# Heads transposed in pairs in a sparse-attention decoder layer, with copies to the other partitions by GpSimd

## The chip, the cores and the metric

One core of a Trainium2 chip runs the kernel. The metric is the device time of one execution in microseconds (us); three executions were timed, and one more was profiled. TensorE is named PE in the profile (PEld its weight loads), VectorE DVE, ScalarE ACT, GpSimd POOL and SyncE SP.

## The reference

One layer on 2048 prompt tokens (16 blocks of 128) and 64 sample tokens, all in float32. Cut to what matters here:

```
z = rmsnorm(x) @ w_in                    # 1024 -> 3656 columns, split into:
q, k, v (8, 4, 4 heads x 64), qi (8 index heads x 64), ki (64), wi (8), ga, u, vm, gm
score[t, l] = sum_h wi[t, h] * relu(qi[t, h] . ki[l])      # causal
idx = top_k(score, 256)                                    # per query
o = softmax(q . k[idx] / 8) @ v[idx];   attn = o * silu(ga)
gm = gelu(u) * (W_s @ layernorm(gelu(vm)) + b) * silu(gm)  # in chunks of 128
r = x + concat(attn, gm) @ w_out
y = r + sigmoid(rmsnorm(r) @ w_ple_gate) * (p @ w_ple_proj)
```

The sample tokens have their keys and values in paged caches. k, v, ki and the sample's normalised vm rows are outputs too.

## The kernel before

float32 products are made of two fp32r parts: `split` has ScalarE copy the value from PSUM into a high part (L124) and VectorE write the rest into a low part (L125). Keys are stacked on the partitions: for 64 dimensions, partitions 0 to 63 hold the high part and 64 to 127 the low part (`ki` for the index, `Kst` for attention). A query head must then lie on both halves. The kernel gets this by doubling before the transpose: each head of 64 columns is loaded twice side by side (`load_qi` for the index, L659; `load_q` for attention, L999), or copied twice by ScalarE (`twice`, L1015, for keys), so that one transpose per head of 128x128 puts it on both halves (L673 for index heads, L1036 for queries, L1021 for keys). Two PSUM tiles of four heads take the eight heads of a block.

The kernel has three phases.

Phase A does the input projection in three rounds of blocks ([0-4 and the sample], [5-10], [11-15]); a round goes through 14 column chunks of w_in and, in each chunk, through its blocks (`proj`, L312 to L322; two PSUM buffers "z"; `post` evacuates them on ScalarE and VectorE). In the first round raw weights are loaded into 5 buffers "raw" (L282), and split by GpSimd ("whi", L288) and VectorE ("wlo", L289); the parts are stored and reloaded in the later rounds. After each product `pump` gives out some steps of index work, within a credit in units of 128 keys: `idx` (queries' transposes, then per 1024 keys and head two matmuls into "dots", a relu on ScalarE L691 and an accumulation on VectorE L693 into "big", which GpSimd first sets to a small descending ramp from a constant `iota`, L679), and `topk`: seven evaluations of a threshold (ScalarE counts over the row, L829; VectorE corrects the threshold, L833 to L849), then VectorE passes over a row and a mask that goes to memory. At most two top-ks and one block of dots are open; the block behind is "primed": its loads are issued. The gMLP half of the output product follows (`gm_product`, L579 to L583, weights "whi" by L302), and in the middle of it (u == 9) the rest of the index work is given out, the pools of the projections are closed, and `prep_early` prepares queries and keys for phase B in between; its transposes use the same two PSUM buffers "tp" as `gm_split` (L567).

Phase B is the attention: blocks 0 to 15, four key heads g each; scores (L1103, L1104), mask and running minimum on VectorE (L1105), exponentials on ScalarE (L1112), transposes of the probabilities (L1138), their split (L124, L125), values (L1155). `prep_q` of the next block runs after g == 2, and the load of the one after that follows it. The sample's attention is interleaved.

Phase C is the output product and the gate. Its weights are loaded and split first (`raw_split`): of the gate's ten parts, GpSimd makes the high part of every third (L1423), and the low part of every third (L1424).

The order within a queue is not the order in which the program gives instructions out: a scheduler places each instruction on its engine's queue by a simulated time line when its operands and buffers are there, with the order of the program as priority. Each engine then works through its queue in that order.

## Time and profile before

| | |
|---|---|
| timed executions | 1889.49, 1889.77, 1900.7 us (median 1889.77) |
| profiled execution | 1893.5 us, of it the span of the core 1891.7 us |
| mean granted clock of TensorE | 0.988 of 2.4 GHz |
| busy: TensorE, VectorE, ScalarE, GpSimd | 1833.5, 1242.1, 1018.2, 623.5 us |
| moved by DMA | 261.53 MB, 83176 of 243806 packets under 512 B |
| phase A, B, C (begin, us) | 0, 1045, 1532 |

The profile is one execution on the chip. "Busy" of TensorE is modelled, since matmuls are pipelined: a duration of 273 ns does not mean that the next one starts 273 ns later. The chain is the work that ended last, followed back from the end. A wait is put down to the instruction that came last.

### The profile page before, as it was taken

What the parts mean: (1) busy time and instruction counts of PE and PEld (TensorE: products, weight loads), DVE (VectorE), ACT (ScalarE), POOL (GpSimd) and SP (SyncE); (2) the same over time, 40 slices, a digit from 0 to 9 for tenths busy, and PEclk for the clock granted to TensorE, in tenths of its full rate; (3) what the DMA queues carried; (4) which work ended last, traced back from release to release, by engine and by line L of the source; (5) the groups of instructions that cost most, each with busy time, mean ns of one, the idle gap of its engine ahead of it and who ended that gap; (6) DMA issues with size and microseconds to landing.
All of it is one profiled execution on the core that took longest, in us unless ns stands there. A gap on an engine that the chain in (4) does not pass through costs nothing.

```text
span 1891.7 us, 33962 instructions
## 1 busy us (share of the span) xinstructions
PE 1833.5 (97%) x11974; PEld 1601.0 (85%) x11974; DVE 1242.1 (66%) x3631; ACT 1018.2 (54%) x1909; POOL 623.5 (33%) x950
## 2 busy tenths in 40 slices
PE   7989998999999999999988899999999999999998
PEld 7989988999999999999877678778777777888887
DVE  5597665378878547788752789888999764233321
ACT  4244335256565636766654888868788653122121
POOL 5482562342012324013303442233221364222221
PEclk9989999999999999999999899999999999999999
DMA  8855756645344554554553442233220373223211
GB/s 253 247 163 179 223 189 203 215 131 161 119 162 146 194 174 145 163 170 134 176 188 128 134 112 76 64 108 94 61 78 12 100 258 122 74 95 104 94 37 45
DMA packets 243806, 261.53 MB, mean 138 GB/s; under 512 B 83176, under 2 KB 209840, under 8 KB 243248
## 3 DMA queue, kind: packets, MB, share of 16 engines
q1 hardware_dynamic: 237744, 240.45, 40.5%
q0 software_dynamic: 5888, 18.88, 3.4%
q8 instruction: 95, 1.56, 0.3%
q14 instruction: 79, 0.65, 0.1%
HBM read 171.90 MB, written 87.37 MB: 137 GB/s over the span
## 4 chain that ended last, share of the span: by engine, by line
PE 83%; DVE 5%; DMA 5%; POOL 2%; issue 2%; ACT 2%; SPq 0%; DVEq 0%; POOLq 0%; ACTq 0%
PE z L319 10%; PE z L320 10%; PE z L322 10%; PE b_o L1155 7%; PE b_tp L1138 6%; PE c_mm L1471 5%; PE c_mm L1470 5%; PE c_mm L1474 5%; PE b_s L1103 3%; PE dots L688 3%; PE dots L689 3%; PE b_s L1104 3%; PE z L579 1%; PE z L580 1%; PE z L583 1%
## 5 line engine op out<-in xcount | busy, mean ns | idle before, releaser
L319 PE MATMUL z<-whi,hhi 128*128 128x256 f32 (+1 forms) x1792 | 463.0, 292 | 10.5 <-ACT vt L414 5.0
L320 PE MATMUL z<-wlo,hhi 128*128 128x256 f32 (+1 forms) x1792 | 454.1, 287 | 0.2 <-DVE wlo L289 0.2
L319 PEld LDWEIGHTS z<-whi,hhi 128*128 128x128 f32 x1792 | 341.9, 191 | 21.2 <-issue 8.5
L320 PEld LDWEIGHTS z<-wlo,hhi 128*128 128x128 f32 x1792 | 341.8, 191 | 6.1 <-DVE wlo L289 1.5
L322 PE MATMUL z<-whi,hlo 128*128 128x256 f32 (+1 forms) x1792 | 262.6, 286 | 0.0
L322 PEld LDWEIGHTS z<-whi,hlo 128*128 128x128 f32 x1792 | 237.7, 190 | 2.0
L693 DVE SCALAR_TENSOR_TENSOR big<-dots,sgn,big 128x1024 f32<-128x1024 f32 (+7 forms) x176 | 179.2, 1018 | 52.3 <-ACT dots L691 50.6
L125 DVE TENSOR_TENSOR b_pt<-b_tp,b_pt 128x512 fp32r<-128x512 f32 (+1 forms) x288 | 183.4, 655 | 12.1 <-ACT b_pt L124 11.0
L691 ACT ACTIVATE dots<-dots 128x1024 f32<-128x1024 f32 (+7 forms) x176 | 140.3, 801 | 87.7 <-PE dots L689 82.9
L1155 PE MATMUL b_o<-b_pt,Vst 128*128 128x512 f32 x544 | 184.1, 424 | 1.2 <-DVE b_pt L125 0.8
L124 ACT ACTIVATE b_pt<-b_tp 128x512 fp32r<-128x512 f32 (+1 forms) x288 | 155.5, 578 | 48.2 <-PE b_tp L1138 45.4
L1138 PE MATMUL b_tp<-mats,b_sm 128*128 128x128 f32 x1088 | 172.0, 275 | 2.3 <-DVE b_pt L125 1.8
L1112 ACT ACTIVATE b_sm<-b_sm,b_st 128x128 f32<-128x128 f32 (+15 forms) x128 | 154.7, 1210 | 16.2 <-DVE b_st L1105 15.4
L829 ACT ACTIVATE bfw<-big,tk 128x384 bf16<-128x384 f32 (+14 forms) x105 | 136.4, 1300 | 45.7 <-DVE tk L849 27.9
L1138 PEld LDWEIGHTS b_tp<-mats,b_sm 128*128 128x128 f32 x1088 | 131.5, 141 | 34.1 <-ACT b_sm L1112 4.8
L1103 PE MATMUL b_s<-Kst,b_qh 128*128 128x512 f32 (+3 forms) x320 | 139.5, 439 | 4.1 <-DVE b_st L1105 2.2
L1105 DVE CUSTOM_DVE_ANT_0 b_sm<-b_s,b_mask,b_st 128x512 f32<-128x512 f32 (+3 forms) x192 | 123.9, 646 | 22.6 <-PE b_s L1104 17.8
L1104 PE MATMUL b_s<-Kst,b_ql 128*128 128x512 f32 (+3 forms) x320 | 117.6, 370 | 0.0
L688 PE MATMUL dots<-ki_stack,qih 128*128 128x512 f32 (+3 forms) x304 | 113.0, 373 | 3.1 <-DVE mk L833 3.1
L689 PE MATMUL dots<-ki_stack,qil 128*128 128x512 f32 (+3 forms) x304 | 110.2, 371 | 0.0
L1471 PE MATMUL c_mm<-c_l_w_ple_gate,c_mh 128*128 128x512 f32 x272 | 106.7, 392 | 3.2 <-DVE c_l_w_ple_gate L1424 2.1
L1470 PE MATMUL c_mm<-c_h_w_ple_gate,c_mh 128*128 128x512 f32 x272 | 109.0, 401 | 0.0
(351 smaller groups left out, 3747.0 us busy)
## 6 DMA issues: line engine op xcount, KB each, us to landing
whi<-s_wh SPq DMA_DIRECT2D x52, 512.0 KB
wlo<-s_wl SPq DMA_DIRECT2D x52, 512.0 KB
raw<-w_in SPq DMA_DIRECT2D x112, 128.0 KB
s_wh<-whi SPq DMA_DIRECT2D x13, 1024.0 KB
s_wl<-wlo SPq DMA_DIRECT2D x13, 1024.0 KB
b_qr<-s_q SPq DMA_DIRECT2D x32, 256.0 KB
s_r<-hlo SPq DMA_DIRECT2D x32, 256.0 KB
c_r<-s_r SPq DMA_DIRECT2D x16, 512.0 KB
```

The lines of the kernel that those rows point to most:

```text
L125: nc.vector.tensor_tensor(lo, src, hi.bitcast(F32), OP.subtract)
L319: nc.tensor.matmul(z, lhsT=hh[:, k], rhs=wh[:, k, :n], start=(k == 0), stop=False)
L320: nc.tensor.matmul(z, lhsT=hh[:, k], rhs=wl[:, k, :n], start=False, stop=False)
L322: nc.tensor.matmul(z, lhsT=hl[:, k], rhs=wh[:, k, :n], start=False, stop=(k == 7))
L688: nc.tensor.matmul(ps[:, s0:s0 + sn], lhsT=qh[h // 4][:, h % 4], rhs=rhs, start=True, stop=False)
L693: nc.vector.scalar_tensor_tensor(a, r, self.sgn[:, b, h:h + 1], a, op0=OP.mult, op1=OP.add)
L1103: nc.tensor.matmul(ps, lhsT=qh[:, h], rhs=rhs, start=True, stop=False)
L1104: nc.tensor.matmul(ps, lhsT=ql[:, h], rhs=rhs, start=False, stop=True)
L1138: nc.tensor.transpose(ps[:, k, r], sm2[r][:, (k0 + k) * 128:(k0 + k) * 128 + 128], ident)
L1155: nc.tensor.matmul(o.rearrange("p a b -> p (a b)"), lhsT=Vst[:, kb, g].rearrange("p a d -> p (a d)"), rhs=pt[:, k].rearrange("p a b -> p ( ...
L1470: nc.tensor.matmul(z, lhsT=hi[:, k], rhs=wts[k][0][:, ns], start=(k == 0), stop=False)
L1471: nc.tensor.matmul(z, lhsT=hi[:, k], rhs=wts[k][1][:, ns], start=False, stop=(b == SB and k == nk - 1))
```

## The change

1. Index queries (`idx`), attention queries (`prep_q`) and keys (`prep_kv`) are loaded once, and two heads of 64 are transposed together (one 128x128 transpose; head 2j on partitions 0 to 63, head 2j+1 on 64 to 127). `heads` splits each half where it lies, and then GpSimd copies it to the other half (four copies of 64 x 512). For query blocks 0 to 4 (`direct`) ScalarE and VectorE write the other half from PSUM as well. For keys, the high part is written on the head's own half and the low part on the other; `twice` is gone. Head h is now `[:, h % 2, h // 2]`.
2. The index queries of the primed block are transposed and split once the running block has done five steps, at no credit. `prep_q` runs after g == 0.
3. When only top-ks are left, their steps take no credit, so `pump` gives them all out at once.
4. The ramp is made for each block by GpSimd's iota and a scaling in place; the constant is gone. "raw" has 4 buffers, and the index key of a token is written once.
5. `prep_early` uses the PSUM buffers "dots". In phase C the gate's weights are split by ScalarE and VectorE alone.

```diff
-            rp = pool("a_raw", 5)
+            rp = pool("a_raw", 4)
...
+                    kin = wk.tile([128, 64], F32, name="kin", bufs=KIN)[:P]
+                    nc.scalar.activation(kin, z[:, 0:64], AF.Copy, scale=rs)
+                    self.rope(nc.vector, kin[:, None, :], rt, 1, wk, P)
...
+                        nc.tensor.transpose(ps[:64, 0], kin, ident)
+                        kst = self.ki[:, b]
+                        nc.scalar.activation(kst[0:64], ps[:64, 0], AF.Copy)
+                        nc.vector.tensor_tensor(kst[64:128], ps[:64, 0], kst[0:64].bitcast(F32), OP.subtract)
+
+                    if b != SB:
+                        later.append(ki_t)
...
+                    if primed and primed[0][0] not in ready and (not dots or steps[0] >= 5):
+                        ready.add(primed[0][0])
+                        if primed[0][0] != SB:
+                            next(primed[0][1])
...
-                            credit[0] -= v
+                            if dots or primed or blocks_due:
+                                credit[0] -= v
...
-                            early = self.prep_early(eb, lambda: self.tp.tile([128, 4, 128], F32, name="tp"))
+                            early = self.prep_early(eb, lambda: self.dp.tile([128, 1024], F32, name="dots")[:, :512]
+                                                    .rearrange("p (a b) -> p a b", a=4))
...
+    def order(self, acc, P):
+        nc = self.nc
+        nc.gpsimd.iota(acc[:P], pattern=[[1, acc.shape[1]]], base=0, channel_multiplier=0,
+                       allow_small_or_imprecise_dtypes=True)
+        nc.gpsimd.tensor_scalar(acc[:P], acc[:P], -UNIT, 1.0, op0=OP.mult, op1=OP.mult)
+
+    def heads(self, pool, names, ps, bufs, direct=False):
+        nc = self.nc
+        qh, ql = (pool.tile([128, 2, 4, 128], F32R, name=n, bufs=bufs) for n in names)
+        own = [slice(0, 64), slice(64, 128)]
+        for e in range(2):
+            nc.scalar.activation(qh[own[e], e], ps[own[e]], AF.Copy)
+            nc.vector.tensor_tensor(ql[own[e], e], ps[own[e]], qh[own[e], e].bitcast(F32), OP.subtract)
+            if direct:
+                nc.scalar.activation(qh[own[1 - e], e], ps[own[e]], AF.Copy)
+                nc.vector.tensor_tensor(ql[own[1 - e], e], ps[own[e]], qh[own[e], e].bitcast(F32), OP.subtract)
+        if direct:
+            return qh, ql
+        for t in (qh, ql):
+            for e in range(2):
+                nc.gpsimd.tensor_scalar(t[own[1 - e], e], t[own[e], e].bitcast(F32), 1.0, 1.0, op0=OP.mult, op1=OP.mult)
+        return qh, ql
+
...
     def idx(self, b):
         nc, wk, wk2 = self.nc, self.wk, self.wk2
         W = 128 * (b + 1)
-        qds = self.load_qi(b)
+        qd = wk2.tile([128, 4, 128], F32, name="qid", bufs=2)
+        nc.sync.dma_start(qd, self.s_qi[b].rearrange("p (h d) -> p h d", h=4))
         yield None
-        qh, ql = [], []
-        for j in range(2):
-            qd = qds[j].rearrange("p h a d -> p h (a d)")
-            ps = self.tp.tile([128, 4, 128], F32, name="tp")
-            for h in range(4):
-                nc.tensor.transpose(ps[:, h], qd[:, h], self.ident)
-            qh.append(wk2.tile([128, 4, 128], F32R, name="qih", bufs=3))
-            ql.append(wk2.tile([128, 4, 128], F32R, name="qil", bufs=3))
-            self.split(qh[j], ql[j], ps)
-            yield 2
+        ps = self.tp.tile([128, 4, 128], F32, name="tp")
+        for j in range(4):
+            nc.tensor.transpose(ps[:, j], qd[:, j], self.ident)
+        qh, ql = self.heads(wk2, ("qih", "qil"), ps, 2)
+        yield None
         acc = self.big.tile([128, SEQ], F32, name="big")[:, :W]
-        nc.gpsimd.tensor_scalar(acc, self.iota[:, :W], -UNIT, 1.0, op0=OP.mult, op1=OP.mult)
+        self.order(acc, 128)
...
-            q = io.tile([128, 8, 2, 64], F32, name="b_qr", bufs=1)
+            q = io.tile([128, 4, 128], F32, name="b_qr", bufs=1)
             ga = io.tile([128, 512], F32, name="b_ga")
-            for a in range(2):
-                nc.sync.dma_start(q[:, :, a], self.s_q[i].rearrange("t (h d) -> t h d", h=8))
+            nc.sync.dma_start(q, self.s_q[i].rearrange("t (h d) -> t h d", h=4))
...
-        kds = {}
-
-        def twice(i):
-            kds[i] = raw.tile([128, 4, 2, 64], F32, name="b_kd")
-            nc.scalar.copy(kds[i], kvs[i][0].rearrange("p (h d) -> p h d", h=4)[:, :, None, :].to_broadcast([128, 4, 2, 64]))
-
         def prep_kv(i, psum):
-            k, v = kds.pop(i), kvs.pop(i)[1]
+            k, v = kvs.pop(i)
             ps = psum()
-            for g in range(4):
-                nc.tensor.transpose(ps[:, g], k[:, g].rearrange("p a d -> p (a d)"), ident)
-            ks = Kst[i // 4][:, :, (i % 4) * 128:(i % 4) * 128 + 128]
-            nc.scalar.activation(ks, ps, AF.Copy)
-            V.tensor_tensor(ks[64:128], ps[64:128], ks[64:128].bitcast(F32), OP.subtract)
+            for j in range(2):
+                nc.tensor.transpose(ps[:, j], k[:, j * 128:j * 128 + 128], ident)
+            ks = Kst[i // 4].rearrange("p (j e) n -> p j e n", e=2)[:, :, :, (i % 4) * 128:(i % 4) * 128 + 128]
+            own = [slice(0, 64), slice(64, 128)]
+            for e in range(2):
+                nc.scalar.activation(ks[own[e], :, e], ps[own[e], 0:2], AF.Copy)
+                V.tensor_tensor(ks[own[1 - e], :, e], ps[own[e], 0:2], ks[own[e], :, e].bitcast(F32), OP.subtract)
...
+            ps = psum()
+            for j in range(4):
+                nc.tensor.transpose(ps[:, j], q[:, j], ident)
+            qh, ql = self.heads(qp, ("b_qh", "b_ql"), ps, 2, direct=i < 5)
...
-                if si < len(steps) and g == 2 and at + 1 < NB:
+                if si < len(steps) and g == 0 and at + 1 < NB:
...
-                    raw_split(*gates[q], nc.gpsimd if q % 3 == 2 else nc.scalar, nc.gpsimd if q % 3 == 1 else V)
+                    raw_split(*gates[q], nc.scalar, V)
```

## Rows read from the trace of the kernel before

**Rows 1.** The page: TensorE's busy time, and the chain that ended last by engine.

```profile
PE 1833.5 (97%) x11974; PEld 1601.0 (85%) x11974; DVE 1242.1 (66%) x3631; ACT 1018.2 (54%) x1909; POOL 623.5 (33%) x950
...
PE 83%; DVE 5%; DMA 5%; POOL 2%; issue 2%; ACT 2%; SPq 0%; DVEq 0%; POOLq 0%; ACTq 0%
```

**Rows 2.** Busy time by stretch: PE, PEld, DVE, ACT, POOL; granted clock, DMA share, GB/s.

```profile
0.00:320.00 320.00, 298.71 (x2152) 273.57 (x2153) 209.33 (x747) 127.83 (x285) 163.19 (x277) 0.97 0.68 210
320.00:660.00 340.00, 338.06 (x2585) 328.47 (x2584) 239.67 (x877) 193.11 (x362) 88.25 (x168) 1.00 0.50 160
660.00:980.00 320.00, 319.52 (x2211) 296.39 (x2210) 227.06 (x662) 203.38 (x287) 80.60 (x129) 1.00 0.53 166
980.00:1045.00 65.00, 51.62 (x249) 41.33 (x247) 22.72 (x49) 27.37 (x51) 18.02 (x32) 0.92 0.37 120
1045.00:1110.00 65.00, 59.62 (x366) 48.17 (x366) 52.44 (x179) 54.94 (x163) 33.02 (x66) 0.92 0.47 130
1110.00:1530.00 420.00, 416.36 (x2781) 326.55 (x2779) 369.20 (x987) 330.31 (x632) 130.58 (x204) 1.00 0.28 81
1530.00:1580.00 50.00, 44.73 (x211) 35.46 (x210) 31.49 (x28) 19.78 (x29) 34.60 (x22) 1.00 0.65 234
```

**Rows 3.** Chain of waits by line: 320:660, 700:980, 980:1045, 1045:1110, 1110:1520, 1530:1580.

```profile
by line: PE z L319 25.6%; PE z L320 25.5%; PE z L322 25.5%; PE dots L689 6.5%; PE dots L688 6.5%; DMA s_q<-qn 2.4%; PE tp L250 2.2%; PE tp L673 1.5%; PE tp L338 1.5%; ACT bfw L829 0.4%; DVE big L693 0.3%; PE tp L366 0.3%; PE z L312 0.3%; AC
...
by line: PE z L322 18.4%; PE z L319 18.2%; PE z L320 18.0%; PE dots L689 10.6%; PE dots L688 10.4%; PE z L579 4.7%; PE z L580 4.6%; PE z L583 4.6%; ACT bfw L829 1.9%; PE tp L567 1.6%; PE tp L338 1.5%; PE tp L673 1.2%; issue 0.8%; DVE big L8
...
by line: PE z L579 20.4%; PE z L580 19.6%; PE z L583 16.4%; DMA b_kr<-k_prompt 9.0%; PE tp L1021 8.1%; DVE Kst L1024 4.3%; ACT hlo L585 2.9%; ACT Kst L1023 2.8%; DVE v L865 2.7%; DVE big L863 2.7%; PE tp L567 2.7%; issue 2.3%; DVE bfw L875 
...
by line: PE b_o L1155 15.9%; PE b_tp L1138 14.9%; PE b_s L1103 11.6%; DMA b_qr<-s_q 10.2%; PE b_s L1104 9.6%; PE b_tp L1036 7.0%; PE b_o L1179 4.4%; issue 4.1%; ACT b_sm L1112 3.3%; DVE b_pt L125 3.2%; PE b_tp L1304 3.0%; ACT b_pt L124 2.0%
...
by line: PE b_o L1155 27.1%; PE b_tp L1138 24.8%; PE b_s L1103 13.9%; PE b_s L1104 12.5%; DVE b_sm L1105 3.9%; PE b_tp L1359 3.8%; PE b_tp L1304 2.8%; PE b_s L1313 2.2%; PE b_o L1179 2.1%; PE b_tp L1036 1.9%; DVE b_pt L125 1.1%; issue 1.0%;
...
by line: POOL c_l_w_ple_gate L1424 16.2%; POOL c_x L1437 14.3%; DMA c_r<-s_r 13.4%; PE c_mm L1474 10.1%; issue 9.7%; PE c_mm L1471 8.3%; PE c_mm L1470 7.3%; POOL c_st L1495 7.1%; POOL c_st L1496 3.3%; PE c_tp L1454 2.0%; POOL c_h_w_ple_gate
```

**Rows 4.** Groups by line: the index transposes (busy, mean ns, idle before).

```profile
L673 PE MATMUL tp<-mats,qid 128*128 128x128 f32 x112 | 17.5, 273 | 1.2 <-DVE wsS L641 0.7 <-DMA qid<-s_qi 0.5
```

**Rows 5.** Groups by line and form: GpSimd's iota and its copy of 128x512.

```profile
L754 POOL TENSOR_SCALAR qid<-sraw 128x512 f32<-128x512 f32 x8 | 5.6, 701 | 12.5 <-PE tp L786 5.3 <-PE z L312 5.1 <-DMA sraw<-cache_idx_k,prow 2.1
...
L512 POOL IOTA iota<- 128x2048 int16 x1 | 1.8, 1837 | 0.4 <-POOLq L1578 0.4
```

**Rows 6.** Groups by line: the split of the queries.

```profile
L125 DVE TENSOR_TENSOR b_ql<-b_tp,b_qh 128x512 fp32r<-128x512 f32 x30 | 20.3, 684 | 0.5 <-ACT b_qh L124 0.3
...
L124 ACT ACTIVATE b_qh<-b_tp 128x512 fp32r<-128x512 f32 x30 | 17.7, 611 | 7.2 <-PE b_tp L1036 7.0
```

**Rows 7.** TensorE's waits, 980:1062: total us, times, longest.

```profile
PE tp L1021 <- DVE Kst L1024: 7.3, 2, 6.2
PE tp L567 <- DVE Kst L1024: 3.4, 3, 1.8
PE b_tp L1036 <- DMA b_qr<-s_q: 2.0, 1, 2.0
```

**Rows 8.** The low parts of phase C's weights (ns min/median/max).

```profile
L1424 DVE TENSOR_TENSOR c_l_w_ple_gate<-c_raw,c_h_w_ple_gate x5: 1214/1219/3385, 1540.5 to 1559.7; 128x1024 fp32r<-128x1024 f32 x5
...
L1424 POOL TENSOR_TENSOR c_l_w_ple_gate<-c_raw,c_h_w_ple_gate x3: 2372/2413/3385, 1545.6 to 1563.7; 128x1024 fp32r<-128x1024 f32 x3
```

**Rows 9.** ScalarE in order of time, 950:966 (start, us).

```profile
957.05 1.58 ACT L829 ACTIVATE bfw<-big,tk 128x1536 bf16<-128x1536 f32 x1
...
958.61 0.60 ACT L585 ACTIVATE hlo<-z 128x512 f32<-128x512 f32 x1
960.49 1.58 ACT L829 ACTIVATE bfw<-big,tk 128x1536 bf16<-128x1536 f32 x1 [1.28 <-DVE tk L849]
```

**Rows 10.** SyncE's queue waits, 0:320: total us, times, longest.

```profile
SPq L282 <- DVE wlo L289: 19.9, 25, 3.4
SPq L659 <- PE tp L673: 16.0, 2, 8.1
```

More of the change, by code (lines that the diff above doesn't have):

```diff
@@ L446, in phase_a @@
             blocks_due, dots, tops = [], [], []
-            primed, active, steps = [], [None], [0]
+            primed, active, steps, ready = [], [None], [0], set()
             credit, turn = [0.0], [0]
@@ L745, in sample_idx @@
         acc = self.big.tile([128, SEQ], F32, name="big")
+        self.order(acc[:, :WS], 64)
         pgs = {}
@@ L770, in third @@
             if p == 3:
-                V.scalar_tensor_tensor(acc[:64, c * 512:c * 512 + n], self.iota[:64, c * 512:c * 512 + n], -UNIT,
-                                       scs.pop(c)[:64, :n], op0=OP.mult, op1=OP.add)
+                a = acc[:64, c * 512:c * 512 + n]
+                V.tensor_tensor(a, scs.pop(c)[:64, :n], a, OP.add)
         for c in range(3):
@@ L1030, in prep_q @@
             q, ga = qs.pop(i)
-            qh = qp.tile([128, 8, 128], F32R, name="b_qh")
-            ql = qp.tile([128, 8, 128], F32R, name="b_ql")
-            for j in range(2):
-                ps = psum()
-                for h in range(4):
-                    nc.tensor.transpose(ps[:, h], q[:, j * 4 + h].rearrange("p a d -> p (a d)"), ident)
-                self.split(qh[:, j * 4:j * 4 + 4], ql[:, j * 4:j * 4 + 4], ps)
+            ps = psum()
+            for j in range(4):
+                nc.tensor.transpose(ps[:, j], q[:, j], ident)
+            qh, ql = self.heads(qp, ("b_qh", "b_ql"), ps, 2, direct=i < 5)
             stt = tiny.tile([128, 8, 6], F32, name="b_st")
```

35 lines of the change are left out of this document (10 added, 25 removed).

## Prediction

> **What bounds the kernel now.** I read the page first: TensorE is busy 97% of the span and holds 83% of the chain that ended last [rows 1]. That share is a mean over stages, so next I cut the span into stages [rows 2] and then asked, stage by stage, for the chain of waits [rows 3]. In the rows of 320 to 660 and 1110 to 1530 TensorE has no idle time worth naming, at a granted clock of 1.00 (2.4 GHz): what leaves its queue there comes off the end. In three short stages it does have idle time: 13.4 us of 65 at 980 to 1045 (the tail of phase A, where keys are prepared for phase B), 5.4 of 65 at 1045 to 1110 (the small query blocks), 5.3 of 50 at 1530 to 1580 (the weights of phase C); in the first two the granted clock also averages 0.92, so part of the time is at 1.2 GHz. The first round, 0 to 320, has 21.3 us idle. TensorE's "busy" is modelled, so I use the chain's shares rather than busy sums.
>
> **The change, part by part.**
>
> *Fewer transposes.* 4 go in each of 14 index blocks, 4 in each of 16 query blocks, 2 in each of 16 key blocks: 152. One lasts 273 ns [rows 4], but they are pipelined, and what counts is their share of the chain [rows 3]. At 320 to 660 the index transposes hold 1.5% of 340 us, 5.1 us for 48 of them, 0.106 us each; half go: 2.55. At 700 to 980, 1.2% of 280 is 3.4; half: 1.7. Block 15 lies between: 4 x 0.106 = 0.4. The three blocks of the first round are not counted. Keys: 8.1% of 65 is 5.3; half: 2.6. Queries: 7.0% of 65 is 4.55; half: 2.3; and 1.9% of 410 is 7.8; half: 3.9. Sum 13.4 us. If another engine takes the place of TensorE, half of it, 6.7, is the lower end.
>
> The Trainium skill, "TensorE: Matmul & The Clock Gate", Part 4 (PE-mode transpose), gives about 275 ns for a transpose in a kernel's context, much of it access latency. The row's 273 ns agrees with that as a duration, not as a price; taken as a price it is a rival below.
>
> *Queries' copies.* The ScalarE and VectorE passes keep their number (two and two per block, now on 64 partitions with the same 512 elements). Four GpSimd copies of 64x512 are new. The nearest row is the 128x512 copy, 0.70 us [rows 5]; both differ in partitions, and no row here shows GpSimd writing other partitions than it reads, so 0.4 to 1.4 us each (from half a row to two), 0.7 taken: 2.8 us per block. Blocks 5 to 15 share 420 us, and the copies are for the next one, so they are hidden; without that cover the block's first scores would wait those 2.8 us. Queued behind them on GpSimd are the ropes, the norms' powers and the next accumulator; none of these is among the lines of the chain from 320 to 980 [rows 3]. In query blocks 0 to 4 the copies are done directly: two more ScalarE passes of 0.61 us and two more VectorE passes of 0.68 us [rows 6] in blocks 1 to 4, 4.9 and 5.5 us in a stage where those engines are busy 54.9 and 52.4 of 65 us [rows 2]. Nothing if they find gaps, 5.5 if they don't: loss 2.5, the middle.
>
> *Query loads.* One DMA takes the place of two, and with the preparation moved from g = 2 to g = 0 the next load is issued half a block earlier. The load holds 10.2% of 65 us, 6.6, on the chain at 1045 to 1110 [rows 3], while TensorE itself idles 2.0 for it [rows 7]. Gain 2.0 to 6.6; nearer the wait itself: 3. SyncE's queue is also freed: it stood 16.0 us at index loads that waited for transposes in the first round [rows 10].
>
> *Tail of phase A.* TensorE waits 7.3 us for the key subtraction to free "tp" for key transposes and 3.4 for the same before the gm transposes [rows 7]. VectorE is late since the last top-k and the flag stand ahead. The change gives the key transposes the "dots" buffers, so the gm transposes no longer share; takes away 16 ScalarE copies ("twice"), and gives the last top-ks out earlier. But an evaluation of the last top-k follows the one before at 3.44 us, 1.58 of it ScalarE and the rest mainly VectorE's steps [rows 9]: a chain that emission can't shorten; and the accumulator is now set by iota and a scaling rather than by the scaling alone, at 0.9 ns per element of iota (1.84 us for 2048 [rows 5]), 1.4 us at 1536 and again before the blocks that wait for its buffer. TensorE's queue still stops at the third key transposes if VectorE is late. So between 0 and 13.4; I take 5, the 3.4 and part of the rest.
>
> *Phase C.* At 1530 to 1580 the chain goes through GpSimd; its low halves of w_ple_gate hold 16.2% of 50 us, 8.1 [rows 3]. Three such passes and three high ones go to VectorE and ScalarE; on VectorE one takes 1.22 us against 2.41 [rows 8]. TensorE has only 5.3 us to win here; the adds of x and r and their DMA stay on the chain: 3.5, between 0 and 5.3.
>
> The longest VectorE pass took 3.39 us, not 1.22 [rows 8]. The Trainium skill, "SBUF — State Buffer", section "Who interferes with whom", says why it may: a VectorE instruction with two SBUF inputs and a GpSimd one that reads SBUF exclude each other. GpSimd's adds stay, so by that rule the new passes may take 3.39 each, and this gain is 0 rather than 3.5.
>
> *First round.* One raw weight buffer less: SyncE stood 19.9 us in 25 waits for a free one [rows 10]; a quarter more is 5. GpSimd gets some 10 us more (three blocks of copies and iotas, one iota for the sample) beside 163 busy of 320 [rows 2]. Against that go the 16.0 us of SyncE. From 6 lost to 5 won; 0 taken.
>
> *Last top-ks at once; the index key's single copy; the sample's buffers.* The first moves emission only; the second saves one narrow pass per block off the chain; the third swaps buffers within one block: 0.
>
> Sum: 13.4 - 2.5 + 3 + 5 + 3.5 = 22.4 us. The profiled execution took 1893.5 (span 1891.7); the median of the runs is 3.7 lower. 1889.8 - 22.4 gives 1867.4.
>
> **Rivals.**
> (a) TensorE's saving turns into waits for others. For it: VectorE is busy 369 of 420 us at 1110 to 1530 [rows 2]. Against: the lines of TensorE in the chain there add up to 91% [rows 3]. Then phase A's 4.65, 2 of the loads and 1.5 of phase C stand against 5.5 for direct copies: 2.7 won, 1887.
> (b) Tail, loads and phase C come back whole: 13.4, 6.6 and 5.3 instead of 5, 3 and 3.5, 13.8 more: 1853.6. For it: separate PSUM buffers. Against: the top-k chain's fixed 3.44 us.
> (c) A transpose costs its whole duration: 152 x 0.273 = 41.5 instead of 13.4: 1839. Against: the shares of the chain.
> (d) Slower: the last two top-ks, given out in one go, fill ScalarE's queue, and the projections' evacuations stand behind them. Seven evaluations and the passes behind them, taken as ten steps of 3.44 us, are 34; the two z buffers cover two projections (24 matmuls each, at 338 us for 2585 [rows 2], 3.1 us), 6.3; each round's end costs 28, three cost 84: 1895 to 1951. It decides once an evacuation waits over 6.3 us. Against: queue order is not emission order; between two evaluations ScalarE does the gm product's copy [rows 9].
>
> **How the numbers follow.** Forecast 1867 (own range 1858 to 1878): 0.46. (a) 0.30, (b) 0.12, (c) 0.05, (d) 0.07. Under 1%, 18.9 us, is about what a measurement of this kernel cannot tell from no change. Faster by more means under 1871: 0.31 of the forecast, (b) and (c): 0.48. Within 1%: the forecast's other 0.15, (a), and 0.01 of (d) if one end alone is hit, less what rounding takes: 0.45. Slower: 0.07. All upper bounds together give 1846, all lower ones 1893 (6.7 + 2 - 5.5 - 6 is 2.8 lost). The range 1848 to 1893 holds the forecast, (a) and (b), 0.88, less a little for their edges.
>
> **What would show it.** Right: half as many index, query and key transposes, with half their chain share; no TensorE wait for "b_qr"; gm transposes no longer waiting for the key subtraction; no GpSimd split on the chain after 1530. Wrong: a cross-partition GpSimd copy far over 1.4 us, so that scores wait for it; ScalarE evacuations queued behind evaluations at round ends, with TensorE waiting for z; more idle TensorE in the first 320 us, at "raw" or "whi"; a last top-k that ends later than 985 us and a tail still over 13 us idle.

## The result, and the profile after the change

The changed kernel takes 1916.25 us (median of four, 1914.44 to 1918.82); the kernel before, on the same chip, 1889.63. The ratio is 1.0123, with a 95% interval of 1.0102 to 1.0144. The forecast was 1867 with a range of 1848 to 1893: the change makes the kernel slower by 1.2% (the two medians alone stand 26.6 us, 1.4%, apart), on the side that had a chance of 0.07. The profiled execution has a span of 1917.0 us, against 1891.7. Two executions far outside all others, one of the experiment e15 at 3568 us and one of the kernel before at 2235 us, are left out of the ratios.

The page of the changed kernel, its line of busy times, and the busy time by stretch (columns as in [rows 2]):

```profile
PE 1830.5 (95%) x11821; PEld 1590.3 (83%) x11821; DVE 1264.8 (66%) x3659; ACT 1024.0 (53%) x1921; POOL 691.4 (36%) x1059
```

```profile
0.00:320.00 320.00, 287.64 (x2055) 262.72 (x2056) 208.34 (x736) 122.69 (x275) 169.50 (x295) 0.94 0.65 199
320.00:660.00 340.00, 337.83 (x2589) 326.99 (x2588) 239.95 (x859) 195.76 (x361) 107.52 (x184) 1.00 0.50 161
660.00:980.00 320.00, 304.76 (x2117) 284.97 (x2116) 221.01 (x611) 183.37 (x264) 109.20 (x166) 0.97 0.44 143
980.00:1045.00 65.00, 65.00 (x314) 53.58 (x313) 32.57 (x127) 37.05 (x66) 12.33 (x23) 1.00 0.57 191
1045.00:1110.00 65.00, 47.30 (x247) 35.33 (x246) 50.23 (x156) 52.12 (x145) 31.56 (x61) 0.84 0.39 120
1110.00:1530.00 420.00, 414.34 (x2757) 322.52 (x2755) 370.66 (x1002) 332.79 (x650) 152.67 (x252) 1.00 0.23 72
1530.00:1580.00 50.00, 47.02 (x235) 36.83 (x234) 34.29 (x53) 28.54 (x45) 24.56 (x22) 0.97 0.63 224
```

TensorE has 153 instructions less than in [rows 1] and its busy time is down by 3.0 us, but its idle time is up: by 11.1 us in the first 320, by 14.8 at 660 to 980, by 12.3 at 1045 to 1110. In the tail, 980 to 1045, the 13.4 us of idle time of [rows 2] are gone. The stretches are the same microseconds in both traces, although the changed kernel is up to 24 us late in them; for the tail, shifted stretches are compared below. GpSimd is busy 68 us longer.

To place the loss I took the same instruction in both traces (same engine, operation and names, same number counted from the front) and subtracted its start in the trace before from its start after. "Late" is in us; the place is the time before.

| kernel | round 2 begins, 334 | last round begins, 646 | its "vm" columns, 677 | its "q" columns, 719 | last key columns, 878 | last mask pass, 1519 | TensorE's end, 1885 |
|---|---|---|---|---|---|---|---|
| after the change | 9.9 | 8.5 | 18.0 | 13.4 | 24.4 | 20.1 | 25.6 |

So there are four places: the first round (+10), the step from x1, x2 to vm in the last round (+9.5), the q and k columns of the last round (+11), phase C (+5.5). Between them 10.3 us are won.

*The last round's first columns.* VectorE, GpSimd, SyncE and again VectorE, then TensorE of the changed kernel, 658 to 678, and the busy times of 677 to 687 (columns as in [rows 2]):

```profile
658.97 0.41 DVE L379 TENSOR_TENSOR qn<-z,absw 128x256 f32<-128x256 f32 x1
...
663.18 1.74 POOL L668 IOTA big<- 128x1920 f32 x1 [2.08 <-DVE kin L136]
664.88 0.89 POOL L133 TENSOR_TENSOR rope_t<-qn,ropet 128x32 f32<-128x32 f32 x1
...
666.50 1.81 POOL L670 TENSOR_SCALAR big<-big 128x1920 f32<-128x1920 f32 x1
668.38 0.61 POOL L135 TENSOR_TENSOR qn<-qn,ropet 128x64 f32<-128x64 f32 x2
668.95 0.60 POOL L136 TENSOR_TENSOR qn<-qn,rope_t 128x64 f32<-128x64 f32 x2
...
666.59 1.03 SPq L276 DMA_DIRECT2D wlo<-s_wl  x2
667.71 1.01 SPq L276 DMA_DIRECT2D whi<-s_wh  x2
669.29 1.48 SPq L382 DMA_DIRECT2D s_qi<-qn  x2
...
676.79 0.75 DVE L379 TENSOR_TENSOR qn<-z,absw 128x256 f32<-128x256 f32 x2 [4.63 <-DMA s_qi<-qn]
...
677.26 0.58 PE L319 MATMUL z<-whi,hhi 128*128 128x256 f32 x1 [5.73 <-DVE qn L379]
...
677.00:687.00 10.00, 9.73 (x59) 9.74 (x60) 1.39 (x4) 0.00 (x0) 3.58 (x14) 0.68 0.13 41
```

Read it from below. TensorE waits 5.73 us for a z buffer, which VectorE frees when it copies z to "qn"; VectorE waits 4.63 for a "qn" buffer, which is free once its store to "s_qi" has landed; the store was issued at 669.29, behind four loads of weights of 512 KB each, and VectorE goes on 7.5 us after that. It was issued so late, 10.3 us after VectorE began to write this "qn" (658.97), since the rope of "qn" on GpSimd (L133 to L136) stands around the iota and the scaling of the next block's ramp, 1.74 and 1.81 us, and behind the iota's own wait of 2.08. Seen from TensorE the wait has the names of VectorE and a DMA; the cause is three queues away. It costs more than the wait: after it, from 677 to 687, the mean granted clock is 0.68, so part of that time is at 1.2 GHz (0.32 of 10 us, an estimated 3.2 us, is lost by it), where the kernel before has 1.00 from 320 to 980 [rows 2].

In the kernel before, a store that stands behind four such loads makes VectorE wait as well, but the store is issued 1.9 us after VectorE began to write its "qn" (660.20), VectorE waits 3.23 us for it, and TensorE doesn't wait there:

```profile
660.20 0.42 DVE L379 TENSOR_TENSOR qn<-z,absw 128x256 f32<-128x256 f32 x1
...
661.71 0.32 POOL L136 TENSOR_TENSOR qn<-qn,rope_t 128x64 f32<-128x64 f32 x1
...
662.14 0.38 SPq L382 DMA_DIRECT2D s_qi<-qn  x1
...
668.85 0.42 DVE L379 TENSOR_TENSOR qn<-z,absw 128x256 f32<-128x256 f32 x1 [3.23 <-DMA s_qi<-qn]
```

*The q and k columns.* ScalarE, VectorE, SyncE and TensorE, 857 to 880:

```profile
857.28 0.46 ACT L393 ACTIVATE qn<-z,rs 128x256 f32<-128x256 f32 x1
...
872.05 1.02 ACT L713 ACTIVATE dots<-dots 128x1024 f32<-128x1024 f32 x1
878.93 0.47 ACT L393 ACTIVATE qn<-z,rs 128x256 f32<-128x256 f32 x1 [5.86 <-DVE tk L841]
...
871.63 0.21 DVE L136 TENSOR_TENSOR qn<-qn,rope_t 128x64 f32<-128x64 f32 x1
...
868.51 0.91 SPq L276 DMA_DIRECT2D wlo<-s_wl  x2
870.37 0.91 SPq L276 DMA_DIRECT2D whi<-s_wh  x2
871.87 0.33 SPq L401 DMA_DIRECT2D s_q<-qn  x1
...
879.46 0.58 PE L319 MATMUL z<-whi,hhi 128*128 128x256 f32 x1 [7.69 <-ACT qn L393]
```

VectorE is busy 19.83 of the 20 us from 860 to 880, GpSimd 15.58: a top-k's last passes, another's first, accumulations, the split of index heads and the norms of q come together there. The row puts ScalarE's wait down to a step of a top-k, but the copy at 878.93 is the fourth into three "qn" buffers, and the first of them, written at 857.28, is free only when its store has landed. That store is issued at 871.87, when VectorE has done the last step of the rope, and behind four loads of weights. It is the same chain as in the x columns, with the rope on VectorE.

The other traces agree. In all eleven kernels (the changed one and ten of the experiments below) that lose 8 us or more between 719 and 878, the first rope of these columns ends 12.4 to 15.9 us after ScalarE's copy, its store is issued behind three or four loads of the next column's weights, and the fourth copy comes 6.6 to 9.3 us after the store. In the seven other experiments with a row in the second table, which lose less than 2 us, and in the kernel before, the rope ends after 8.5 to 11.3 us, the store goes out ahead of these loads, and the fourth copy comes 1.8 to 4.0 us after it.

*The first round.* SyncE's waits up to 320, against [rows 10]: the wait for a free raw buffer rose from 19.9 us in 25 times to 36.3 in 32 and another 13.8 in 4 (the second row names a step of a top-k, which does not use the raw weights: a wait is put down to whatever came last).

```profile
SPq L282 <- DVE wlo L289: 36.3, 32, 5.6
SPq L282 <- DVE tk L872: 13.8, 4, 12.0
```

*Index work of the last round, and the begin of phase B.* SyncE's waits at 690 to 712 and its queue, VectorE, then TensorE's waits at 1045 to 1110:

```profile
SPq L693 <- DMA s_qi<-qn: 6.2, 1, 6.2
```

```profile
700.53 5.62 SPq L693 DMA_DIRECT2D qid<-s_qi  x4
...
1020.51 1.01 DVE L898 TENSOR_SCALAR bfw<-big,tk 128x1536 bf16<-128x1536 f32 x1
...
1023.82 0.75 DVE L1042 TENSOR_TENSOR Kst<-dots,Kst 64x256 fp32r<-64x256 f32 x2 [0.37 <-ACT Kst L1041]
```

```profile
PE b_s L1115 <- DVE b_st L1117: 6.9, 6, 4.2
PE dots L1037 <- DMA b_kr<-k_prompt: 5.0, 2, 2.6
```

The first load of index queries in the last round goes out at 700.5 (668.7 before), the first index dots start at 708.6 (679.8 before; 18.0 of these 28.8 us is how late the kernel already is at 677), the mask of the last top-k ends at 1021 (984 before), and only then are keys prepared. From the last key columns to a mask pass of the small blocks, 878 to 1127 before and 902.4 to 1148.3 after, TensorE's idle time is 19.0 and 19.2 us:

```profile
878.00:1127.00 249.00, 229.97 (x1308) 192.28 (x1308) 161.90 (x516) 167.85 (x352) 80.80 (x149) 0.96 0.48 146
```

```profile
902.40:1148.30 245.90, 226.66 (x1269) 185.97 (x1268) 175.48 (x549) 175.61 (x370) 89.42 (x157) 0.96 0.44 143
```

The tail's idle time is not saved, it has moved to the begin of phase B, where the granted clock averages 0.84.

*Phase C.* The low parts of the gate's weights on VectorE (ns min, median, max), against [rows 8], and one of them beside GpSimd's addition:

```profile
L1436 DVE TENSOR_TENSOR c_l_w_ple_gate<-c_raw,c_h_w_ple_gate x8: 1207/1212/3442, 1564.8 to 1586.2; 128x1024 fp32r<-128x1024 f32 x8
```

```profile
1576.35 3.02 POOL L1449 TENSOR_TENSOR c_x<-c_x,c_r 128x1024 f32<-128x1024 f32 x1 [0.57 <-DMA c_r<-s_r]
...
1577.01 3.44 DVE L1436 TENSOR_TENSOR c_l_w_ple_gate<-c_raw,c_h_w_ple_gate 128x1024 fp32r<-128x1024 f32 x1
```

*The operations themselves* cost what the prediction took, or a little less. Index transposes (272 ns each, [rows 4] 273) and GpSimd's copies to other partitions (615 ns; 0.7 us was taken from [rows 5]), ns min, median, max:

```profile
L697 PE MATMUL tp<-mats,qid x56: 270/272/327, 76.8 to 806.6; 128*128 128x128 f32 x56
```

```profile
L686 POOL TENSOR_SCALAR qih<-qih x28: 612/615/956, 79.7 to 871.7; 64x512 fp32r<-64x512 f32 x28
...
L686 POOL TENSOR_SCALAR b_qh<-b_qh x22: 613/617/619, 1119.0 to 1449.2; 64x512 fp32r<-64x512 f32 x22
```

### The profile page after: what moved, and what is told of

Read it like the earlier page. It is cut to its first block, busy times and chain, and to the rows that moved or that the text cites. A ratio compares the mean times of both kernels' runs of the same rounds, so it can differ in the third digit from the quotient of the medians.

```text
span 1917.0 us, 33784 instructions
## 1 busy us (share of the span) xinstructions
PE 1830.5 (95%) x11821; PEld 1590.3 (83%) x11821; DVE 1264.8 (66%) x3659; ACT 1024.0 (53%) x1921; POOL 691.4 (36%) x1059
## 5 line engine op out<-in xcount | busy, mean ns | idle before, releaser
L319 PE MATMUL z<-whi,hhi 128*128 128x256 f32 (+1 forms) x1792 | 463.6, 292 | 20.7 <-ACT qn L393 12.1
L319 PEld LDWEIGHTS z<-whi,hhi 128*128 128x128 f32 x1792 | 344.4, 192 | 30.3 <-ACT qn L393 13.8
L1115 PE MATMUL b_s<-Kst,b_qh 128*128 128x512 f32 (+3 forms) x320 | 138.9, 437 | 10.5 <-DVE b_st L1117 8.5
L1117 DVE CUSTOM_DVE_ANT_0 b_sm<-b_s,b_mask,b_st 128x512 f32<-128x512 f32 (+3 forms) x192 | 123.9, 645 | 23.4 <-PE b_s L1116 18.7
```

Of the source, the lines that this page charges most:

```text
L319: nc.tensor.matmul(z, lhsT=hh[:, k], rhs=wh[:, k, :n], start=(k == 0), stop=False)
L1115: nc.tensor.matmul(ps, lhsT=qh[:, r, g], rhs=rhs, start=True, stop=False)
```

## The experiments

The theories: (1) GpSimd's queue. What the change adds there (iota, scaling, copies) delays ropes and norms, then stores, then z. (2) The rival (d) of the prediction: top-ks given out at once. (3) VectorE is the bound. (4) Losses with places of their own: the raw pool, the one load of index queries, phase C. Medians in us; ratios to the kernel before on the same chip, with their 95% intervals. The runs stand on several chips (e1 to e4 on one, e5 to e8, e9 to e12, e13 to e16, e17 and e18), and the kernel before has medians from 1889.6 to 1892.8 there; so where two runs of different chips are compared, some 3 us of the difference tell nothing.

| run | median | ratio | | run | median | ratio |
|---|---|---|---|---|---|---|
| after | 1916.25 | 1.0123 [1.0102, 1.0144] | | e9 | 1904.61 | 1.0067 [1.0050, 1.0084] |
| e1 | 1916.68 | 1.0134 [1.0118, 1.0151] | | e10 | 1892.89 | 1.0002 [0.9993, 1.0012] |
| e2 | 1904.63 | 1.0076 [1.0059, 1.0093] | | e11 | 1900.68 | 1.0044 [1.0028, 1.0061] |
| e3 | 1899.84 | 1.0044 [1.0027, 1.0061] | | e12 | 1883.94 | 0.9958 [0.9942, 0.9975] |
| e4 | 1908.44 | 1.0096 [1.0080, 1.0113] | | e13 | 1909.00 | 1.0101 [1.0084, 1.0118] |
| e5 | 1908.35 | 1.0090 [1.0060, 1.0121] | | e14 | 1874.96 | 0.9915 [0.9899, 0.9932] |
| e6 | 1911.74 | 1.0110 [1.0080, 1.0141] | | e15 | 1873.75 | 0.9914 [0.9898, 0.9931] |
| e7 | 1895.37 | 1.0027 [1.0012, 1.0042] | | e16 | 1898.81 | 1.0048 [1.0030, 1.0065] |
| e8 | 1888.14 | 0.9984 [0.9969, 0.9999] | | e17 | 1870.29 | 0.9891 [0.9874, 0.9909] |
| | | | | e18 | 1883.58 | 0.9955 [0.9940, 0.9969] |

How late each is at the places of the table above:

| run | 334 | 646 | 677 | 719 | 878 | 1519 | 1885 |
|---|---|---|---|---|---|---|---|
| e1 | 10.7 | 9.2 | 17.2 | 12.0 | 22.5 | 18.7 | 23.8 |
| e2 | 4.2 | -0.5 | 9.7 | 4.5 | 14.2 | 5.1 | 10.0 |
| e3 | 7.7 | 3.2 | 5.0 | 0.4 | 10.5 | 8.8 | 7.1 |
| e4 | 5.9 | 5.2 | 7.5 | 3.6 | 13.0 | 11.4 | 14.3 |
| e5 | 5.2 | 3.6 | 11.5 | 9.2 | 18.1 | 6.0 | 10.8 |
| e6 | 7.6 | 6.2 | 15.4 | 10.4 | 21.2 | 17.8 | 17.8 |
| e7 | 2.6 | -1.1 | 0.8 | -5.1 | 10.3 | 0.1 | 3.3 |
| e8 | 4.5 | 0.7 | 2.3 | 0.0 | -0.1 | -11.2 | -7.5 |
| e9 | -4.8 | -6.6 | 3.2 | 3.4 | 5.1 | 10.9 | 10.9 |
| e10 | 4.6 | 1.0 | 2.6 | 1.1 | 9.3 | -1.2 | -0.8 |
| e11 | 5.4 | 2.2 | 4.4 | 2.1 | 1.8 | 8.3 | 6.6 |
| e12 | 8.6 | 5.2 | 7.1 | 4.9 | 4.8 | -8.8 | -9.0 |
| e13 | 3.2 | 2.0 | 9.8 | 5.4 | 15.4 | 11.2 | 16.0 |
| e14 | -0.7 | -2.1 | -1.5 | -3.8 | -3.7 | -14.8 | -17.7 |
| e16 | 6.6 | 11.2 | 19.4 | 17.1 | 18.5 | 7.4 | 6.1 |
| e17 | -0.9 | -5.8 | -4.4 | -6.8 | -6.3 | -23.7 | -22.6 |
| e18 | -1.9 | -6.8 | -4.8 | -10.5 | 5.4 | -9.2 | -9.6 |

Two kernels with the same code up to a place still differ there by some us (after and e6 by 3.2 at 878; e8, e11 and e12 by 4.9): one profile each, so less than 5 us in this table tells nothing by itself.

### One part of the change undone

**e1, credit.** The last top-ks are charged again.

```diff
-                            if dots or primed or blocks_due:
-                                credit[0] -= v
+                            credit[0] -= v
```

> The changed kernel, with the steps of the last top-ks charged to the credit again. If the top-ks given out at once block the queues (the rival of the prediction), the idle time of TensorE at 860 to 880 us goes (8 us) and the last mask comes earlier than 1021 us: about 1905. If they are harmless, since at 860 index blocks are still open and the credit is charged anyway, the time stays at 1916 within 4.

1916.68: no difference, at no place. Theory (2) falls.

**e2, not ahead.**

```diff
-if primed and primed[0][0] not in ready and (not dots or steps[0] >= 5):
+if primed and primed[0][0] not in ready and not dots and len(tops) < 2:
```

> The changed kernel, with the index queries transposed and split only when their own block becomes the running one (their load is still issued one block ahead). If the preparation ahead is what displaces other work in VectorE's and GpSimd's queues, the 8 us at 860 to 880 go and the index steps no longer run late: about 1905. If it hides the copies, as the prediction assumed, the first steps of each block now wait for four copies of 0.6 us: 1916 to 1925.

1904.63: the preparation ahead costs 9 to 12 us; by the table 9.0 of 15.6 us are won by the begin of the last round. The 11 us of the q and k columns stay (4.5 to 14.2 late), so the first half of the expectation has the sum right and the place wrong.

**e3, the ramp from a constant.**

```diff
+iota = ac.tile([128, 1024], mybir.dt.int16, name="iota")
+nc.gpsimd.iota(iota, pattern=[[1, 1024]], base=0, channel_multiplier=0)
...
-nc.gpsimd.iota(acc[:P], pattern=[[1, acc.shape[1]]], base=0, channel_multiplier=0,
-               allow_small_or_imprecise_dtypes=True)
-nc.gpsimd.tensor_scalar(acc[:P], acc[:P], -UNIT, 1.0, op0=OP.mult, op1=OP.mult)
+for c in range(0, acc.shape[1], 1024):
+    a = acc[:P, c:min(c + 1024, acc.shape[1])]
+    nc.gpsimd.tensor_scalar(a, self.iota[:P, :a.shape[1]], -UNIT, -UNIT * c, op0=OP.mult, op1=OP.add)
...
-r = wk2.tile([128, 512], F32, name="sr")[:, :n]
+r = kT2[:, 1].rearrange("p a b -> p (a b)")[:, :n]
```

> The changed kernel, with the ramp made from a constant of 1024 integers by a scaling of each 1024 (the constant's room comes from the sample's relu output, which now shares a buffer with its keys). If the iota of 1.5 to 1.9 us per block in GpSimd's queue is what delays the ropes and norms behind it (GpSimd's queue theory), the waits at 660 to 680 shrink and 6 to 12 us come back: 1904 to 1910. If not, 1913 to 1919.

1899.84, 16 us less, more than expected: the largest single part. From 646 to 677 it loses 1.8 instead of 9.5.

**e4, index heads direct.**

```diff
-qh, ql = self.heads(wk2, ("qih", "qil"), ps, 2)
+qh, ql = self.heads(wk2, ("qih", "qil"), ps, 2, direct=True)
```

> The changed kernel, with the other halves of the index queries written from PSUM by ScalarE and VectorE instead of by GpSimd. If GpSimd's copies (four of 0.6 to 0.8 us per block, each behind ScalarE or VectorE) hold up GpSimd's queue, the time falls by 8 to 15 us: 1901 to 1908. If VectorE is what is late at 860 to 880 (it has no idle time there), two more passes of 0.68 us per block make it worse: 1918 to 1928.

1908.44, 8 less. From 646 to 677 it loses 2.3 instead of 9.5; from 719 to 878, where VectorE has no idle time, it loses 9.4, hardly less than the 11.0 of the changed kernel: both answers hold, each in its stage. GpSimd's copies cost where GpSimd has ropes behind them.

**e5, last round descending.**

```diff
-ROUNDS = [[0, 1, 2, 3, 4, SB], [5, 6, 7, 8, 9, 10], [11, 12, 13, 14, 15]]
-DUE = ROUNDS[:2] + [ROUNDS[2][::-1]]
+ROUNDS = [[0, 1, 2, 3, 4, SB], [5, 6, 7, 8, 9, 10], [15, 14, 13, 12, 11]]
+DUE = ROUNDS[:2] + [ROUNDS[2]]
```

> The changed kernel, with the blocks of the last round projected in descending order, so that block 15, whose index scores come first, is also the first whose index queries are in memory. Theory: the one load of all eight heads has to wait for the second half of its block's queries, which in the last round is the round's last product; index work starts some 29 us later there, the last top-k ends 37 us later (1021), the keys for phase B are prepared late, and 10 to 13 us are lost at 1045 to 1080. If so, the first index dots of the round come near 690, the last mask near 990, and the time falls by 8 to 12: 1904 to 1908. If the late top-k costs nothing, 1913 to 1919.

1908.35, 8 less. The first index dots of the round start at 692 (708.6), the last mask ends at 1007 (1021; near 990 was expected), keys are prepared from 1010 (1024), and from 878 to 1519 the kernel wins 12.1 instead of 4.3. The load that waits for the round's last store is a cause of its own.

**e6, phase C as before.**

```diff
-raw_split(*gates[q], nc.scalar, V)
+raw_split(*gates[q], nc.gpsimd if q % 3 == 2 else nc.scalar, nc.gpsimd if q % 3 == 1 else V)
```

> The changed kernel, with the gate's weights of phase C split as before (a third of the high and of the low parts on GpSimd). The low passes on VectorE took 1.2 or 3.4 us, and from the last mask to the end it took 371.0 us instead of 365.5. If the passes that meet a GpSimd addition are the cost, 365 to 366 us again and 1910 to 1912 in all. If the order of the products is the cost, 1916.

1911.74; from the last mask pass to the end 365.5 us, as before (371.0 after). The five low passes that stay on VectorE take at most 1.70 us:

```profile
L1436 DVE TENSOR_TENSOR c_l_w_ple_gate<-c_raw,c_h_w_ple_gate x5: 1212/1221/1700, 1562.4 to 1580.4; 128x1024 fp32r<-128x1024 f32 x5
```

Over all kernels the stretch takes 362.6 to 369.2 with the old split (eleven kernels, the one before among them) and 368.4 to 371.0 with the new one (seven), but 363.8 in e3: some 4 us, and not by the split alone.

**e13, five raw buffers.** `rp = pool("a_raw", 5)`, with e3's sharing for the room.

> The changed kernel with five buffers for raw weights, as before the change (the room comes from the sample's relu output). The first round is 9.5 us late at the begin of the second in the changed kernel. If SyncE's waits for a free buffer are the cost, some 5 of these come back: 1909 to 1912. If the index work beside it is, 1914 to 1918.

1909.00. At 334 the kernel is 3.2 late instead of 9.9: the raw buffer is 6.7 of the first round's 10.

### One part alone, and one cost doubled

**e9, the ramp alone in the kernel before.**

```diff
-        nc.gpsimd.tensor_scalar(acc, self.iota[:, :W], -UNIT, 1.0, op0=OP.mult, op1=OP.mult)
+        self.order(acc, 128)
```

> The kernel before, with one part of the change alone: the ramp of each index block made by GpSimd's iota and a scaling in place (the constant stays for the sample). If the iota's time in GpSimd's queue is a cost of its own, 8 to 16 us more than before: 1898 to 1906. If it costs only together with GpSimd's copies of the heads, within 3 of before.

1904.61, against 1892.77 of the kernel before there: 0.67% slower without any copy of heads by GpSimd. It is 4.8 early at 334, loses 9.8 from 646 to 677, at the same wait as the changed kernel, and 5.8 from 878 to 1519 (TensorE's waits at 645 to 680, then at 980 to 1045). There the last top-k is 12 us late, and TensorE's longest wait for key preparation grows from the 6.2 of [rows 7] to 14.9:

```profile
PE z L319 <- DVE qn L379: 5.0, 2, 4.5
```

```profile
PE tp L1027 <- DVE Kst L1030: 14.9, 1, 14.9
```

**e16, the ramp twice.** e12 (below), each scaling from the constant done twice.

```diff
+            for _ in range(2):
                 nc.gpsimd.tensor_scalar(a, self.iota[:P, :a.shape[1]], -UNIT, -UNIT * c, op0=OP.mult, op1=OP.add)
```

> e12_copies_in_b with every scaling of the ramp done twice (the second pass writes the same values), so that a ramp takes as long on GpSimd as the iota and its scaling did. If GpSimd's time ahead of the ropes is the cost of the ramp: 8 to 14 more, 1892 to 1898. If the iota costs by where it is placed (one more wait for a free buffer, two pieces between the steps of a rope), and not by its length: 1882 to 1888.

1898.81 against 1883.94: 15 us. It is 2 earlier than e12 at 334, loses 8.0 more than e12 from there to 646, and 6.3 more in the next 31. So the iota is not special: the time that GpSimd spends ahead of the ropes is the cost, and theory (1) holds for the ramp. The sizes go together: e3 takes 16.6 us of ramp off GpSimd and wins 16.4, e9 adds 18.0 and loses 11.8, e16 adds 21.9 and loses 14.9. (The wait for a free buffer ahead of the ramp is nothing new: GpSimd stood there for 82.8 and 54.6 us in the kernel before as well.)

### Combinations

**e7, constant ramp and direct index heads.** e3 and e4 together.

> The changed kernel, with both of GpSimd's additions in the index blocks taken away: the ramp from a constant (e3_const_ramp: 16.5 us less) and the other halves by ScalarE and VectorE (e4_idx_direct: 8 less). If both act by the load of GpSimd's queue, they overlap and the sum is less than 24: 1895 to 1900. If they act on different waits they add: 1890 to 1893. If VectorE becomes the bound, 1900 to 1906.

1895.37. The two seem to overlap (16 and 8 give 21), as one queue's load does, but 3 us between runs of different chips does not show it. Up to 719 the kernel is ahead of the one before by 5 us; in the q and k columns it loses 15.

**e8, constant ramp, descending, phase C as before.** e3, e5 and e6 together.

> The changed kernel with the constant ramp, the last round in descending order and the old split of phase C. If the three losses lie in different stages, they add: 1916 - 16.5 - 10 - 5 = 1884, which is faster than the kernel before by 5. If the late index work of the last round was part of what the constant ramp gave back, 1890 to 1894.

1888.14, between the two answers. The q and k columns lose nothing now.

**e10, e8 with direct index heads.**

> Constant ramp, index heads' other halves by ScalarE and VectorE, last round in descending order, old split of phase C. e7_const_direct reached the last key projections of the last round 10 us late, all of it lost after 719 us; up to 676 it was level with before. If descending order takes that loss away as it did in e8_const_desc_c, 1876 to 1882. If VectorE's extra passes cost as much as GpSimd's copies did, 1886 to 1890, as e8_const_desc_c.

1892.89, above both answers: no gain over e8. From 719 to 878 it loses 8.2 where e8 lost none: with GpSimd relieved of the ramp, VectorE's extra passes cost as much as GpSimd's copies.

**e11, e8 with the buffers "tp".**

```diff
-            early = self.prep_early(eb, lambda: self.dp.tile([128, 1024], F32, name="dots")[:, :512]
-                                                    .rearrange("p (a b) -> p a b", a=4))
+            early = self.prep_early(eb, lambda: self.tp.tile([128, 4, 128], F32, name="tp"))
```

> e8_const_desc_c with the preparation of phase B on the PSUM buffers tp, as before the change. In e8_const_desc_c TensorE does not wait in the tail, but idles 7.3 us in the first 20 us of phase B at a granted clock of 0.64. If the buffers dots only move the idle time from the tail to the begin of phase B, the time stays within 3 of e8_const_desc_c (1888). If the tail's waits come back on top, 1893 to 1900.

1900.68, 12.5 more than e8. The tail's wait is back in one piece of 12.2 us ("issue" means that the profile shows nothing that TensorE waited for): the buffers "dots" are a gain of 12 here. In the changed kernel it does not appear; the late top-ks probably hide it, but no run has the buffers "tp" in that kernel.

```profile
PE tp L1040 <- issue: 12.2, 1, 12.2
```

**e12, e8 with GpSimd's copies for all query blocks.** `self.heads(qp, ("b_qh", "b_ql"), ps, 2)`.

> e8_const_desc_c with GpSimd's copies for all query blocks of phase B, none direct. If the direct passes on ScalarE and VectorE (both busy over 17 of 20 us at 1040 to 1080 there) are what is late in the first blocks, 3 to 6 less: 1882 to 1885. If not, the copies, 2.4 us in a row, come late for the short blocks: 1888 to 1893.

1883.94, 4 less than e8, and 0.42% below the kernel before. Between 878 and 1519, where the edit acts, the profiles differ by 2.5 us (13.6 won instead of 11.1), which is within their scatter. So in phase B, without ropes and norms, GpSimd's copies are no dearer than the direct passes even for the short blocks; that they are cheaper is not shown.

**e14, e12 with five raw buffers** (the constant cut to 512 integers).

> e12_copies_in_b with five raw buffers (the constant cut to 512 integers to make room, so up to four scalings per ramp). e12_copies_in_b is 8 us late at the begin of the second round. If the raw buffer is the cause: 1878 to 1881. If not: 1882 to 1886.

1874.96, 9 less than e12 (6.4 less if each is taken against the kernel before on its chip); at 334 it is 9.3 earlier.

**e15, e12 with e2's edit.**

> e12_copies_in_b with the index queries prepared only when their block becomes the running one. On the changed kernel that alone gave 12 us. If preparing ahead costs in itself: 1874 to 1880. If it cost only because GpSimd's queue was full of ramps: 1882 to 1886; if it hides the copies, as the prediction held, 1886 to 1892.

1873.75, 10 less than e12 (8 by the ratios): preparing ahead costs without the new ramps too. (Its profile is of the execution that is left out of the ratio, so it has no row in the second table.)

**e17, e14 with e2's edit.**

> e14_best_raw5 (1875) with the index queries not prepared ahead, which gave 10 to 12 us twice. If the five raw buffers and the preparation act on different waits: 1863 to 1868. If both gave back the same time (GpSimd's queue in the first round): 1871 to 1875.

1870.29, 1.09% below the kernel before. Busy time by stretch of e17:

```profile
0.00:320.00 320.00, 296.58 (x2141) 270.68 (x2142) 211.79 (x758) 132.20 (x290) 174.72 (x298) 0.97 0.66 209
...
660.00:980.00 320.00, 320.00 (x2191) 296.00 (x2190) 232.65 (x669) 204.13 (x288) 96.32 (x153) 1.00 0.49 159
980.00:1045.00 65.00, 56.45 (x272) 44.71 (x272) 33.20 (x119) 37.50 (x106) 35.44 (x64) 0.87 0.48 154
1045.00:1110.00 65.00, 62.95 (x402) 49.70 (x402) 59.14 (x178) 59.52 (x157) 41.01 (x76) 1.00 0.33 101
```

The time lies between the ranges of the two answers. By the medians 9 and 10 give 14, by the ratios 8 and 8 give 13: the raw buffer and the preparation overlap in part, if at all.

**e18, e17 with the last round ascending again.**

> e17_all_best with the last round in ascending order again, so that only parts of the change itself are left in it: pairs with GpSimd's copies in index and attention, one load, the buffers dots, the early load of queries, the last top-ks at once; the ramp from a constant, the raw buffers, the preparation and phase C as before the change. If the late index work of the last round costs what it did on the changed kernel, 8 more than e17_all_best: 1872 to 1882. If that loss needed GpSimd's full queue, within 3 of it. By the terms of the prediction that this kernel still has (13.4 for the transposes, 3 for the loads, 5 for the tail), it should stand 21 below before, near 1869.

1883.58, 13 more than e17 and above both answers: the order of the last round is worth 13 us with one load for all eight heads. Of these, 11.7 are lost by 878, in the q and k columns. With only parts of the change in it, in the change's own order, the kernel is 0.45% faster than the one before, some 8 us, where the prediction's terms gave 21.

## Why the prediction was wrong

The step that failed is the one on the copies' cover: "the copies are for the next one, so they are hidden", with the ropes, the norms' powers and the next accumulator queued behind them, none of these "among the lines of the chain from 320 to 980". From a chain without GpSimd I took it that GpSimd had slack. It had, on the average (88 of 340 us busy, [rows 2]), but its queue is in order and so is SyncE's: a store that is issued 10.3 us after its "qn" is begun, instead of 1.9, and lands some 7 us later, is more than three "qn" and two z buffers cover. The ramp, which I counted in the tail and as load in the first round, costs 16 us in the changed kernel (e3), 12 alone (e9), 15 when doubled elsewhere (e16); the copies of the index heads 8 (e4; nothing once the ramp comes from a constant and the last round descends, e10); the preparation ahead, which I gave no price at all, 8 to 12 (e2, e15). Undone one at a time, the ramp, the preparation, the raw pool, phase C, the direct copies and the last round's order come to 52 us, undone together (e17, which keeps the index copies) to 46; that agrees with some overlap in one queue but does not show it clear of noise.

Point by point:

- *Transposes, 13.4.* The number was right, their price not everywhere. In phase A e17 is 6.3 early after the last key columns, where 4.65 was taken. In the steady part of phase B (3.9 taken) hardly anything is won: at a mask pass at 1127 of before e17 is 24.5 early and at the last one 23.7, the changed kernel 21.3 and 20.1 late. VectorE is busy 371 of 420 us there, as rival (a) said.
- *Direct copies, 2.5 lost.* 4 by the medians, 2.5 between 878 and 1519 (e8 against e12), neither clear of the scatter.
- *Query loads, 3, and the tail, 5.* No wait for "b_qr" shows among TensorE's waits in the changed kernel, as predicted (1.0 us in e17). The tail was under-sized: from the last key columns to 1127 e17 wins 18.2 us, where keys, first queries, loads and tail were given 12.9, and the buffers "dots" alone are worth 12.5 (e11). In the changed kernel only 3.1 of it arrives, since the last top-k ends at 1021 instead of the 984 of before. That was named as a sign of error ("later than 985"), but for the iota's sake. The larger cause I missed: one load for the two halves of a block's index queries must wait for the store of the second half, and block 15, whose index work comes first, has its x2 as the last product of these columns. Before, the load of x1's half went out alone, at 668.7.
- *Phase C, 3.5 won.* 5.5 lost in the first profile, some 4 over all kernels (e6). The passes took 1.21 us or up to 3.44 us beside GpSimd's addition: the one at 1577.01 ends 1.1 us after that addition does, and two others of 3.4 us (1564.76, 1586.17) stand on the chain that ended last. The bound was set at 0 won; it had to reach below nothing. The Trainium skill, "SBUF — State Buffer", section "Who interferes with whom", says that a VectorE instruction with two SBUF inputs contends with a GpSimd instruction that reads SBUF; the trace agrees (3.44 against 1.21 us).
- *First round, 0.* 10 lost. The raw buffer was priced at 5 and measured at 6.7 (e13) and 9.3 (e14); the 16.0 us of SyncE's waits that were set against it gave nothing back. The sum of SyncE's waits is no price here: for the loads of raw weights (L282) it is 59 us before, 93 after and 101 in e14, which is not late at 334.
- *Last top-ks at once, 0.* Right (e1), and so rival (d), the only slower one, was wrong in its mechanism: the slowdown came from elsewhere.

The sum of the terms, 22.4, is near what e17 shows, some 21 less than the kernel before, with the ramp, the raw pool, the preparation, phase C and the direct copies undone and the last round in descending order. That is luck in good part: the tail gave more than its term, the steady part of phase B and phase C nothing, and 13 us of it need the last round's new order, which is not in the change; in the change's own order 8 are left (e18).

Not settled: the q and k columns of the last round lose 9 to 16 us in every ascending kernel that has the new heads (e9, without them, loses 1.7), and 8 to 9 in two of the descending ones (e5, e10). The traces show in each of them the late rope and the store behind weights that are told above; why VectorE comes to this rope late is argued only. It has no idle time there in the changed kernel, which agrees with a pile-up of late index work, but no run took one piece of it away alone. The scheduler also places instructions anew with every edit; e3's phase C (363.8) is an example of a gain that no edit explains.

## What to carry to other kernels

An engine that is not on the chain of waits has no slack to give if a step that frees a buffer stands behind the new work in its queue: follow each such step through its store and the buffers it holds, in us, before calling work hidden. When two loads are merged, ask which of the two sources is ready last. A saved instruction on the busiest engine is worth what the other engines of that stage leave of it, and a combination of undone parts can beat both kernels, as here by 1.1%.
